# Attention's projection as one direct product by blocks of features, with gating by pairs of heads ahead of it

## Chip, cores and metric

One core of one Trainium2 chip runs the program. The time is device time in microseconds, the median of three runs. The float32 inputs and outputs lie in the chip's memory; every large product is made on TensorE in three parts (high by high, high by low, low by high, "fp32r"), so each operand is split beforehand into a high part (a rounded copy, ScalarE) and a low part (what is left, VectorE or GpSimd).

## Reference

The layer is cut to the part at its end. `y_a` is the MLP branch and `y_b` attention over 8 heads of 128 features:

```python
    y_b = mixture_of_dilations(q, k, v).reshape(B, S, D_B)
    y_b = y_b * jax.nn.silu(z_b)                 # z_b: gating
    m = g_a * (y_a @ w_pa) + g_b * (y_b @ w_pb)  # two projections, [1024 x 2048] and [1024 x 1024]
    return x + rms_norm(m @ w_o, g_post)         # output, [1024 x 1024]
```

Sequence 1024, width 1024. `y_b @ w_pb` is what the change computes in another way.

## The kernel before

The program runs through stages: the norm and V, the other input projections with the MLP's mixing, attention head by head with the MLP's projection interleaved, and a tail. Only the tail is touched.

**Names.** Tiles are 128 partitions by features or tokens. `y` is attention's output times the gate, by features: 8 heads of 128 features (k), two column halves b of 512 tokens. `o_d` holds attention's output and `z_d` the gate in memory, `th_d` the sigmoid gates, `ma_d` the MLP's gated projection, `wo_d` the parts of `w_o` split early. `wh` and `wl` are high and low parts of weights (eight buffers each, `WB`), `wr` raw weights (three buffers). `split` (L158 to L160) makes a high part on ScalarE (ACT) and a low one, on VectorE (DVE) unless told otherwise; `operand` (L103 to L109) does so for weights, low on GpSimd (POOL). `steps` is a generator that issues the rest of the MLP's projection (`pa`, L844 to L846, then `tha` on L850), a quarter of a product at a time.

**The tail before.** Its pool `tail` lies in the memory that attention's pools gave up. `load_y` (L903) loads a quarter of y (four heads, one half, 1 MB) and z in two pieces into `wr` buffers, and multiplies them on POOL (L910). `load_w` loads quarters of `w_pb`. The product is then made from seven smaller ones instead of eight (the Winograd form of Strassen's scheme): sums of quarters of weights and of y (`by_k`, L919, on DVE), seven products of 4 banks x 4 k x 3 matmuls (L1031 to L1033, tiles `pbp`), and corrections between their results (L1041). The operands of product n + 1 are made while product n runs. `gated` (L980 to L988) takes a finished bank: times th on DVE, plus ma on POOL, split into `mh` and `ml`. `load_o` loads the split output weights behind products p5 and p4 and at the end: half of them into y's and the weights' tiles, the others into `wh` and `wl` buffers. The output (L1079 to L1086) runs over pairs of chunks of 128 tokens, with both column halves i of each.

**What sets the order.** Each engine works through its own list in order, and so does SyncE (SP), which issues nearly all transfers: one that waits (for a buffer, or for a store that must land) holds those behind it. The lists come from the order of the code and from a scheduler that may move an instruction past others on its engine; a tile's buffer is given to the next tile once all that read it are done.

Of the kernel before, what the change touches and what calls it, by code (L numbers as in the profile page):

```python
# [36 lines left out]
def tile_hybrid_encoder(  # L37
# [855 lines left out]

    with tc.tile_pool(name="tail", bufs=1) as tp:
        def whole(tag, name, dtype=F32):
            return tp.tile([P, 4, 512], dtype, tag=tag, name=name)


        y, wq, mh, ml = {}, {}, {}, {}

        def load_y(j, b):  # L903
            bs = slice(512 * b, 512 * (b + 1))
            y[j, b] = t = whole(f"y{j}{b}", f"y{j}{b}")
            nc.sync.dma_start(t, o_d[4 * j:4 * j + 4, :, bs].rearrange("k p n -> p k n"))
            for k in range(0, 4, 2):
                z = wpool.tile([P, 2, 512], F32, tag="wr", bufs=3, name=f"zf{j}{b}{k}")
                nc.sync.dma_start(z, z_d[4 * j + k:4 * j + k + 2, :, bs].rearrange("k p n -> p k n"))
                nc.gpsimd.tensor_tensor(t[:, k:k + 2, :], t[:, k:k + 2, :], z, ALU.mult)  # L910

        def load_w(i, j):
            wq[i, j] = whole(f"q{i}{j}", f"pb{i}{j}")
            nc.sync.dma_start(wq[i, j], w_pb[512 * j:512 * (j + 1), 512 * i:512 * (i + 1)].rearrange(
                "(k p) n -> p k n", p=P))

        def by_k(dst, first, second, op, eng=nc.vector):
            for k in range(4):
                eng.tensor_tensor(dst[:, k, :], first[:, k, :], second[:, k, :], op)  # L919
                yield  # L920

        load_y(0, 0)
        load_w(1, 0)
        load_w(1, 1)
        take(steps, 8)
        load_w(0, 0)
        load_y(1, 1)
        s1, s2 = whole("s1", "s1"), whole("s2", "s2")
        for _ in by_k(s1, wq[1, 0], wq[1, 1], ALU.add):
            take(steps, 2)  # L930
        load_y(0, 1)
        load_w(0, 1)
        for _ in by_k(s2, s1, wq[0, 0], ALU.subtract):
            take(steps, 2)
        load_y(1, 0)
        t3 = whole("t3", "t3")
        for _ in by_k(t3, y[1, 1], y[0, 1], ALU.subtract):
            take(steps, 2)
        for _ in by_k(y[0, 1], y[0, 1], y[0, 0], ALU.subtract):
            take(steps, 2)  # L940
        for _ in by_k(wq[1, 0], wq[0, 0], wq[1, 0], ALU.subtract):
            take(steps, 2)
        take(steps)
        u2, u3 = [hpool.tile([P, 4, 512], F32, tag=t, name=f"u{t}") for t in ("r01h", "r10h")]
        for q_, tag in (((0, 0), "r10l"), ((1, 0), "r01l")):
            ml[q_] = hpool.tile([P, 4, 512], F32R, tag=tag, name=f"ml{tag}")
        sso = tp.tile([P, 8, 4], F32, name="sso")


        t2, t1, t4, w_s3, s4 = y[0, 0], y[0, 1], y[1, 0], wq[1, 0], s2  # L950
        TOKENS = {"p1": y[0, 0], "p6": t2, "p2": y[1, 0], "p7": t3, "p5": t1, "p4": t4, "p3": y[1, 1]}
        WEIGHTS = {"p1": wq[0, 0], "p6": s2, "p2": wq[0, 1], "p7": w_s3, "p5": s1, "p4": wq[1, 1], "p3": s4}
        spare = [(0, 0), (1, 1)]

        def tokens_of(n, hl):
            if n == "p6":
                sums = by_k(t2, t3, y[0, 0], ALU.add)
            elif n == "p4":
                sums = by_k(t4, y[1, 0], t2, ALU.subtract)
            else:  # L960
                sums = iter(())
# [54 lines left out]
        for at, (n, _, _) in enumerate(STEPS):  # L1016
# [7 lines left out]
            for u in range(4):  # L1024
                ps = acc.pop((into, u)) if into else next_bank(f"pb{n}{u}")
                if n in ("p1", "p7", "p5"):
                    acc[n, u] = ps
# [108 lines left out]
```

## Time and profile before

| | us |
|---|---|
| median of three runs | 1615.31 |
| the runs | 1612.32, 1615.61, 1615.31 |
| the profiled execution | 1610.12 |
| its span, first to last instruction | 1608.3 |
| mean granted clock of TensorE | 0.976 |

| part of the tail, us from the span's start | from | to |
|---|---|---|
| last of the MLP's projection (TensorE alone on it) | 1358.95 | 1408.78 |
| attention's projection | 1408.78 | 1499.33 |
| output | 1499.33 | 1600.67 |
| last square, scale, sum and store | 1600.67 | 1608.3 |

In rows of a view, an engine stands ahead of its line of the code, the operation and what it writes and reads; "[... <-X]" is the time that the engine sat idle before, and what ended it. PE is TensorE, SPq the time in which SP held a transfer's instruction.

### The profile page before, as it was taken

The page shows a single profiled execution, that of the slowest core. Times are in us where ns is not written, and L with a number is a line of the kernel's source. Part 1 is how long each engine was busy: PE and PEld are TensorE (multiplying, and loading weights), DVE is VectorE, ACT ScalarE, POOL GpSimd, SP SyncE. Part 2 cuts the span into 40 slices and gives each one's busy share as a digit, 9 for nine tenths or more (in the row PEclk, how much of TensorE's full clock was granted, in tenths as well). Part 3 has the DMA queues.
Part 4 walks back from the last instruction along what each step waited for, and adds up shares of the span by engine and source line. Part 5 has one row for each costly group of instructions (what it writes and reads, how often), then busy time and mean ns, then how long its engine had stood idle before and what let it go on. Part 6 is the DMA issues. An engine that isn't in the chain of part 4 may idle for free.

```text
span 1608.3 us, 22594 instructions
## 1 busy us (share of the span) xinstructions
PE 1508.8 (94%) x7751; PEld 1264.2 (79%) x7751; DVE 934.6 (58%) x1698; ACT 716.0 (45%) x1391; POOL 818.5 (51%) x723
## 2 busy tenths in 40 slices
PE   8959999999999999999999999989998899789798
PEld 4747999988888888788788888767877777677586
DVE  5852544476675765757565655566666554596412
ACT  5422533343433434443354544677776665144111
POOL 3542644465555555565555555364344433687432
PEclk8979999999999999999999999999999999999899
DMA  8335433334534443536243343676666665924631
GB/s 263 136 125 191 150 106 105 111 125 133 162 125 144 135 147 116 180 102 193 99 159 130 121 148 110 217 227 196 194 198 179 207 188 168 334 97 144 235 105 66
DMA packets 238467, 252.14 MB, mean 157 GB/s; under 512 B 14056, under 2 KB 174856, under 8 KB 238096
## 3 DMA queue, kind: packets, MB, share of 16 engines
q1 hardware_dynamic: 238128, 250.14, 48.8%
q8 instruction: 61, 1.00, 0.3%
q10 hardware_dynamic: 224, 0.56, 0.1%
q14 instruction: 54, 0.44, 0.1%
HBM read 174.10 MB, written 76.55 MB: 156 GB/s over the span
## 4 chain that ended last, share of the span: by engine, by line
PE 63%; DVE 13%; DMA 6%; ACT 6%; issue 6%; POOL 5%; SPq 1%; DVEq 0%; POOLq 0%; ACTq 0%
PE sg L515 2%; PE pa L845 1%; PE pa L844 1%; PE pa L846 1%; DMA wr_pa<-in_w_proj_a_dram 1%; DMA vn<-v_d 1%; DVE vn L504 1%; PE vb L154 1%; PE vb L156 1%; PE vb L155 1%; PE sc L650 1%; ACT st L657 1%; DVE y L919 1%; ACT qrh L159 1%; PE pr L731 1%
## 5 line engine op out<-in xcount | busy, mean ns | idle before, releaser
L108 POOL TENSOR_TENSOR wl_pa<-wr_pa,wh_pa 128x512 fp32r<-128x512 f32 x56 | 73.4, 1318 | 86.7 <-ACT wh_pa L106 69.4
L504 DVE TENSOR_SCALAR vn<-vn,mean,rstd 128x128 f32<-128x128 f32 x128 | 55.3, 486 | 34.9 <-DMA vn<-v_d 34.5
L657 ACT ACTIVATE st<-st,own 128x256 f32<-128x256 f32 (+1 forms) x128 | 63.0, 493 | 24.0 <-DVE own L653 23.4
L106 ACT ACTIVATE wh_pa<-wr_pa 128x512 fp32r<-128x512 f32 x64 | 38.7, 624 | 46.1 <-DMA wr_pa<-in_w_proj_a_dram 37.2
L671 POOL COPY oth<-own 32x4 f32<-32x4 f32 x128 | 25.1, 196 | 54.1 <-ACT st L657 49.8
L653 DVE CUSTOM_DVE_ANT_0 st<-sc,tb 128x256 f32<-128x256 f32 x64 | 25.6, 422 | 37.8 <-PE sc L652 27.4
L160 POOL TENSOR_TENSOR vl<-vn,vh 128x512 fp32r<-128x512 f32 x32 | 41.3, 1292 | 0.8 <-ACT vh L159 0.8
L1085 ACT ACTIVATE sq<-o 128x512 f32<-128x512 f32 x16 | 9.6, 599 | 70.5 <-PE o L1083 70.5
L160 POOL TENSOR_TENSOR qcl<-q,qch 128x512 fp32r<-128x512 f32 x16 | 24.8, 1552 | 29.7 <-ACT qch L159 29.6
L1061 DVE TENSOR_TENSOR sso<-sso 128x1 f32<-128x1 f32 x8 | 1.3, 159 | 63.5 <-ACT sq L1085 63.5
L159 ACT ACTIVATE mhp<-mb 128x512 fp32r<-128x512 f32 x16 | 10.1, 632 | 54.9 <-POOL mb L987 54.9
L160 DVE TENSOR_TENSOR vl<-vb,vh 128x512 fp32r<-128x512 f32 x16 | 10.8, 688 | 38.2 <-ACT vh L159 33.9
L165 POOL TENSOR_TENSOR sso<-sso,mhalf 128x1 f32<-128x1 f32 x8 | 4.4, 552 | 54.9 <-DVE sso L164 54.9
L108 POOL TENSOR_TENSOR wl_wos<-wr_wos,wh_wos 128x512 fp32r<-128x512 f32 x16 | 20.7, 1293 | 22.8 <-ACT wh_wos L106 22.8
L154 PE MATMUL vb<-wh_vb,hT00h 128*128 128x512 f32 x32 | 14.2, 445 | 18.7 <-DVE vl L160 18.7
L1081 PE MATMUL o<-woh,mhp 128*128 128x512 f32 x64 | 26.3, 414 | 5.8 <-DMA woh<-wo_h 5.8
L987 POOL TENSOR_TENSOR mb<-thb,mb 128x512 f32<-128x512 f32 x16 | 21.4, 1337 | 19.8 <-DVE thb L986 15.5
L160 DVE TENSOR_TENSOR ptla<-pa,ptha 128x512 fp32r<-128x512 f32 (+1 forms) x32 | 19.8, 618 | 17.7 <-ACT ptha L159 17.6
L910 POOL TENSOR_TENSOR y<-y,zf 128x1024 f32<-128x1024 f32 x8 | 24.0, 3006 | 11.5 <-DMA zf<-z_d 8.7
L1082 PE MATMUL o<-wol,mhp 128*128 128x512 f32 x64 | 26.8, 422 | 3.1 <-DMA wol<-wo_l 3.1
L650 PE MATMUL sc<-krh,qch 128*128 128x256 f32 (+2 forms) x80 | 24.3, 306 | 5.7 <-DVE own L653 5.2
L653 DVE CUSTOM_DVE_ANT_0 st<-sc,ta 128x256 f32<-128x256 f32 x48 | 20.0, 420 | 15.2 <-PE sc L652 7.3
(2695 smaller groups left out, 6073.0 us busy)
## 6 DMA issues: line engine op xcount, KB each, us to landing
wr_pa<-in_w_proj_a_dram SPq DMA_DIRECT2D x32, 512.0 KB, 5.4
wr_g<-in_w_in_dram SPq DMA_DIRECT2D x16, 512.0 KB, 3.8
wr_va<-in_w_in_dram SPq DMA_DIRECT2D x16, 512.0 KB, 3.8
wr_u<-in_w_in_dram SPq DMA_DIRECT2D x16, 512.0 KB, 3.7
wr_z<-in_w_in_dram SPq DMA_DIRECT2D x16, 512.0 KB, 4.2
vn<-v_d SPq DMA_DIRECT2D x32, 256.0 KB, 3.1
y_d<-s SPq DMA_DIRECT2D x32, 256.0 KB, 2.5
wr_yf<-y_d SPq DMA_DIRECT2D x16, 512.0 KB, 5.1
```

What stands on the lines that cost most here:

```text
L106: nc.scalar.activation(hi, src, AF.Copy)
L108: low.tensor_tensor(lo, src, f32(hi), ALU.subtract)
L154: nc.tensor.matmul(ps, lhs[k][0], rh, start=(k == 0), stop=False)
L159: nc.scalar.activation(hi, src, AF.Copy)
L160: low.tensor_tensor(lo, src, f32(hi), ALU.subtract)
L504: nc.vector.tensor_scalar(vn[:, c, :], vn[:, c, :], mean[:, 4 * b + c, 0:1], rstd[:, 4 * b + c:4 * b + c + 1], op0=ALU.subtract, op1=ALU.mult)
L515: nc.tensor.matmul(pg[:, 256 * c:256 * (c + 1)], w[:, 2 * cp + c, :], wst, start=(w is vh and c == 0), stop=(w is vl and c == 1), skip_gro ...
L650: nc.tensor.matmul(dst, lhs[0], rhs[0], start=True, stop=False)
L653: nc.vector.tensor_tensor_reduce(st[:, t, :n], ps[:, t, :n], bias, -1.0, -NEG, ALU.add, ALU.min, own[:, half, idx, 0:1])
L657: nc.scalar.activation(st[:, t, :n], st[:, t, :n], AF.Exp, bias=own[:, half, idx, 0:1], scale=-1.0, accum_out=own[:, half, idx, 1:2])
L1081: nc.tensor.matmul(ps, mhi, wh, start=(k == 0), stop=False)
L1082: nc.tensor.matmul(ps, mhi, wl, start=False, stop=False)
```

## The change

The seven products become one direct product, by blocks of 128 output features (m = 0 to 7) and two column halves: 16 banks of 8 k x 3 matmuls. The weights of a block are loaded whole (8 x 128 x 128, rows of 128 columns) by `cols_block`, one block ahead in the code. Ahead of it, `gated_heads` loads o and z for two heads and one half, multiplies on POOL head by head, and splits into tiles of one head each; 16 such steps alternate with four steps of the MLP each. The tiles of o have two buffers, that of z one. The output's first three chunks of weights for column half 0 have tiles of their own; the other five take `wh` and `wl` buffers, and those of half 1 the y tiles of b = 0. The output's loop goes by token half b, then i, then four chunks. The low part of `m` is made on DVE throughout, and the very last store is issued from ACT's queue.

```diff
-        def load_y(j, b):
...
-            y[j, b] = t = whole(f"y{j}{b}", f"y{j}{b}")
-            nc.sync.dma_start(t, o_d[4 * j:4 * j + 4, :, bs].rearrange("k p n -> p k n"))
-            for k in range(0, 4, 2):
-                z = wpool.tile([P, 2, 512], F32, tag="wr", bufs=3, name=f"zf{j}{b}{k}")
...
-                nc.gpsimd.tensor_tensor(t[:, k:k + 2, :], t[:, k:k + 2, :], z, ALU.mult)
...
+        def gated_heads(h, b):
+            bs = slice(512 * b, 512 * (b + 1))
+            o, z = [tp.tile([P, 2, 512], F32, tag=t, bufs=n, name=f"{t}{h}{b}") for t, n in (("o", 2), ("z", 1))]
+            for t, src in ((o, o_d), (z, z_d)):
+                nc.sync.dma_start(t, src[h:h + 2, :, bs].rearrange("k p n -> p k n"))
+            for i in range(2):
+                y[h + i, b] = [tp.tile([P, 512], F32R, name=f"y{s}{h + i}{b}") for s in "hl"]
+                nc.gpsimd.tensor_tensor(o[:, i, :], o[:, i, :], z[:, i, :], ALU.mult)
+                split(*y[h + i, b], o[:, i, :])
                 yield
...
+        ready = (_ for h in range(0, H, 2) for b in range(2) for _ in gated_heads(h, b))
+        for i in range(16):
+            take(ready, 1)
+            take(steps, 4)
+            if i == 8:
+                take(steps, 8)
         take(steps)
...
+                if i == 0 and k > 2:
+                    wo[i, k] = [wpool.tile([P, 512], F32R, tag=f"w{s}", bufs=WB, name=f"wo{s}{k}") for s in "hl"]
                 else:
+                    wo[i, k] = [tp.tile([P, 512], F32R, tag=f"y{s}{k}0" if i else f"wo{s}{k}", name=f"wo{s}{i}{k}")
+                                for s in "hl"]
...
+        wb[0] = cols_block(w_pb, 0, 0, "pb0")
+        for m in range(KT):
+            if m + 1 < KT:
+                wb[m + 1] = cols_block(w_pb, (m + 1) * P, 0, f"pb{m + 1}")
+            if m == 4:
+                load_o(0, range(3))
+            elif m == 7:
+                load_o(0, range(3, KT))
+            for b in range(2):
...
+                ps = next_bank(f"pb{b}{m}")
+                for k, (lh, ll) in enumerate(wb[m]):
+                    rh, rl = y[k, b]
+                    nc.tensor.matmul(ps, lh, rh, start=(k == 0), stop=False)
+                    nc.tensor.matmul(ps, lh, rl, start=False, stop=False)
+                    nc.tensor.matmul(ps, ll, rh, start=False, stop=(k == KT - 1))
+                nc.vector.tensor_tensor(th, th, ps, ALU.mult)
+                nc.gpsimd.tensor_tensor(ma, th, ma, ALU.add)
+                split(*[t[:, m % 4, :] for t in m_[m // 4][b]], ma)
+        load_o(1, range(KT))
...
-        for cc in range(4):
...
+        for b in range(2):
             for i in range(2):
-                for c in (2 * cc, 2 * cc + 1):
...
+                for c in range(4 * b, 4 * b + 4):
```

Left out of it are the removed loads of quarters, sums, products and corrections (`load_w`, `by_k`, `tokens_of`, `weights_of`, `begin`, `gated`) and lines that differ only in names.

How the instructions stand on SP where the tail's loads begin, behind the last stores of attention. Before (names: `y` and `zf` are quarters of o and their gates, `pb` quarters of `w_pb`, `pa161` the MLP's weights; DMAHW is a transfer that must have landed):

```order
L906 DMA y00_13530<-o_d_86 128x4x512 [waits DMAHW6_49,DMAHW0_49,PE_49]
L914 DMA pb10_13538<-in_w_proj_b_dram 128x4x512 [waits DMAHW2_49]
L914 DMA pb11_13540<-in_w_proj_b_dram 128x4x512 [waits DMAHW3_49]
L914 DMA pb00_13578<-in_w_proj_b_dram 128x4x512 [waits DMAHW4_49]
L906 DMA y11_13580<-o_d_86 128x4x512 [waits DMAHW5_49]
L909 DMA zf110_13582<-z_d_91 128x2x512 [waits DMAHW7_49,Pool_49]
L909 DMA zf112_13585<-z_d_91 128x2x512 [waits Pool_49]
L113 DMA wr_pa161_13604<-in_w_proj_a_dram 128x8x128 [waits Pool_49]
```

And of the change, from the same place:

```order
L903 DMA o00_13530<-o_d_86 128x2x512 [waits DMAHW6_49,DMAHW0_49,PE_49]
L903 DMA z00_13531<-z_d_91 128x2x512 [waits DMAHW2_49]
L903 DMA o01_13580<-o_d_86 128x2x512 [waits DMAHW3_49]
L113 DMA wr_pb0_13855<-in_w_proj_b_dram 128x8x128 [waits DMAHW4_49,Pool_49]
L903 DMA z01_13581<-z_d_91 128x2x512 [waits DMAHW5_49,DMAHW2_49,Pool_49]
L903 DMA o20_13632<-o_d_86 128x2x512 [waits DMAHW1_49,DVE_49]
L851 DMA ma_d_95<-tha14_13562 128x512 [waits DMAHW7_49,DVE_49]
L113 DMA wr_pb1_13865<-in_w_proj_b_dram 128x8x128 [waits Pool_49]
L903 DMA z20_13633<-z_d_91 128x2x512 [waits DMAHW5_49,Pool_49]
```

The loads of pa161 and pa171 now stand ahead of the first o; every z from the second on waits for POOL.

On POOL, in the change, around the last pair of heads (`o60` and `o61` are the products for heads 6 and 7, halves 0 and 1; `mb00` adds the MLP's part to the first bank):

```order
L906 TENSOR_TENSOR o41_13790<-o41_13790,z41_13791 128x512
L108 TENSOR_TENSOR wl_pb3_0_14021<-wr_pb3_14017,wh_pb3_0_14019 128x512 [waits DMAHW3_49,PE_49,Activation_49]
L108 TENSOR_TENSOR wl_pb3_1_14025<-wr_pb3_14017,wh_pb3_1_14023 128x512 [waits PE_49,Activation_49]
L906 TENSOR_TENSOR o60_13818<-o60_13818,z60_13819 128x512 [waits DMAHW5_49,DMAHW0_49,DVE_49]
L906 TENSOR_TENSOR o60_13818<-o60_13818,z60_13819 128x512
L962 TENSOR_TENSOR mb00_13877<-thb00_13875,mb00_13877 128x512 [waits DVE_49]
L906 TENSOR_TENSOR o61_13832<-o61_13832,z61_13833 128x512 [waits DMAHW4_49,DMAHW1_49,Pool_49]
```

`mb00`, which needs the whole first bank, stands ahead of the products for heads 6 and 7 of the second half; two low parts of weights stand between pairs. Before, POOL's products y (L910) stood among the low parts of `pa` and `pbp`.

On SP, the output's weights. Before (`woh` and `wol` are high and low parts; `thb` and `mb` belong to the last banks):

```order
L1003 DMA woh3_14452<-wo_h_97 128x512 [waits DMAHW6_49,PE_49]
L1003 DMA wol3_14453<-wo_l_98 128x512 [waits DMAHW7_49,PE_49]
L983 DMA thb010_14471<-th_d_92 128x512 [waits DMAHW0_49,Pool_49]
L985 DMA mb010_14473<-ma_d_95 128x512 [waits DMAHW1_49,Pool_49]
L983 DMA thb011_14492<-th_d_92 128x512 [waits DMAHW2_49,Pool_49]
L985 DMA mb011_14494<-ma_d_95 128x512 [waits DMAHW3_49,DVE_49]
L1003 DMA woh4_14542<-wo_h_97 128x512 [waits DMAHW4_49,PE_49]
```

And of the change, at its last two banks (`woh10` is half 1, chunk 0; `woh00`, the first of half 0, stands 43 rows further up, behind the first th of the second block):

```order
L952 DMA thb07_14429<-th_d_92 128x512 [waits DMAHW3_49,Pool_49]
L938 DMA woh7_14425<-wo_h_97 128x512 [waits DMAHW4_49,PE_49]
L938 DMA wol7_14426<-wo_l_98 128x512 [waits DMAHW5_49,PE_49]
L954 DMA mb07_14431<-ma_d_95 128x512 [waits DMAHW6_49,DVE_49]
L938 DMA wol10_14496<-wo_l_98 128x512 [waits DMAHW7_49,PE_49]
L938 DMA woh10_14495<-wo_h_97 128x512 [waits DMAHW0_49,PE_49]
L952 DMA thb17_14462<-th_d_92 128x512 [waits DMAHW1_49,Pool_49]
L954 DMA mb17_14464<-ma_d_95 128x512 [waits DMAHW2_49,DVE_49]
```

The weights of half 0 have moved from behind the last product to between the banks of the blocks.

More of the change, by code (lines that the diff above doesn't have):

```diff
@@ L912, in load_w @@
[L912 to L919, printed above, removed]
-                yield
[L922 to L940, printed above, removed]
@@ L947, in tile_hybrid_encoder @@
         sso = tp.tile([P, 8, 4], F32, name="sso")
[L950 to L961, printed above, removed]
-            for k in range(4):
-                take(sums, 1)
-                split(hl[0][:, k, :], hl[1][:, k, :], TOKENS[n][:, k, :])
-                yield
@@ L967, in weights_of @@
-        def weights_of(n, res):
-            if n == "p3":
-                take(by_k(s4, wq[0, 1], s2, ALU.subtract))
-            for u in range(4):
-                res.append(operand(WEIGHTS[n][:, :, u * P:(u + 1) * P], f"pb{n}{u}"))
-                yield
-        def begin(n):
-            hl, res = quarter(*spare[0], f"pb{n}"), []
-            spare.reverse()
-            return hl, res, tokens_of(n, hl), weights_of(n, res)
-        def gated(i, b, u, c):
-            bs = slice(512 * b, 512 * (b + 1))
-            th = wpool.tile([P, 512], F32, tag="th", bufs=2, name=f"thb{i}{b}{u}")
-            nc.sync.dma_start(th, th_d[8 + 4 * i + u][:, bs])
-            ma = wpool.tile([P, 512], F32, tag="ws", bufs=2, name=f"mb{i}{b}{u}")
-            nc.sync.dma_start(ma, ma_d[4 * i + u][:, bs])
-            nc.vector.tensor_tensor(th, th, c, ALU.mult)
-            nc.gpsimd.tensor_tensor(ma, th, ma, ALU.add)
-            split(mh[i, b][:, u, :], ml[i, b][:, u, :], ma, nc.vector if u % 2 else nc.gpsimd)
@@ L1054, in tile_hybrid_encoder, with load_o @@
-        load_o(0, range(4, 8))
-        gp = whole("y11", "gp")[:, 0:2, :].rearrange("p k n -> p (k n)")
+        wo = {}
+        def load_o(i, ks):
+            for k in ks:
+                if i == 0 and k > 2:
+                    wo[i, k] = [wpool.tile([P, 512], F32R, tag=f"w{s}", bufs=WB, name=f"wo{s}{k}") for s in "hl"]
+                else:
+                    wo[i, k] = [tp.tile([P, 512], F32R, tag=f"y{s}{k}0" if i else f"wo{s}{k}", name=f"wo{s}{i}{k}")
+                                for s in "hl"]
+                for s in range(2):
+                    nc.sync.dma_start(f32(wo[i, k][s]), wo_d[s][i, k])
@@ L1060, in out_last @@
             nc.sync.dma_start(x_, x_t[c])
+            out_ = tp.tile([P, D], F32, tag="o", bufs=2, name=f"out{c}")
             nc.vector.tensor_tensor(sso[:, c, 2:3], sso[:, c, 0:1], sso[:, c, 1:2], ALU.add)
```

90 lines of the change are left out of this document (16 added, 74 removed).

## The prediction

> **What bounds the kernel now.** I read the page first, then the tail of the program stage by stage, the waits of TensorE (PE) there, and the timeline around the longest of them.
>
> ```profile
> span 1608.3 us, 22594 instructions
> PE 1508.8 (94%) x7751; PEld 1264.2 (79%) x7751; DVE 934.6 (58%) x1698; ACT 716.0 (45%) x1391; POOL 818.5 (51%) x723
> ```
>
> PE bounds the whole, so the tail is counted in matmuls and in the time that PE loses. Nothing before the tail is changed. The stages, on PE: the end of the MLP projection (the first two rows, split where its waits begin), attention's projection, and the output (the last two).
>
> ```profile
> core 0: us, PE busy (x), PEclk, DMA share, GB/s
> 1358.95:1380.73 21.78, 21.78 (x98) 1.00 0.79 281
> 1380.73:1408.78 28.05, 19.66 (x73) 0.88 0.92 313
> 1408.78:1499.33 90.55, 81.65 (x337) 0.96 0.40 131
> 1499.33:1525.00 25.67, 16.85 (x52) 0.80 0.74 259
> 1525.00:1600.67 75.67, 75.66 (x334) 1.00 0.24 80
> ```
>
> ```profile
> 1358.96 0.39 PE L844 MATMUL pa<-ya1000h,wh_pa 128*128 128x512 f32 x1
> 1380.51 0.39 PE L846 MATMUL pa<-ya1111h,wl_pa 128*128 128x512 f32 x1
> ...
> 1393.63 0.79 PE L846 MATMUL pa<-ya1201h,wl_pa 128*128 128x512 f32 x1 [5.13 <-POOL wl_pa L108]
> 1394.22 0.63 PE L844 MATMUL pa<-ya1201h,wh_pa 128*128 128x512 f32 x1
> 1397.64 0.57 PE L846 MATMUL pa<-ya1201h,wl_pa 128*128 128x512 f32 x1
> ...
> 1600.28 0.39 PE L1083 MATMUL o<-woy,mlp 128*128 128x512 f32 x1
> ```
>
> The first two rows are the first and last of 96 matmuls in a row (8 groups of 12): 21.55 us over 95 steps, 0.2268 us each. From 1394.22 to 1397.64, behind the wait of 5.13 us, eight steps take 3.42 us, 0.43 each: after a long wait PE runs at half speed for some 4 us, so it costs about 2 us more than its length.
>
> By the code 168 matmuls of the MLP are left at 1358.95, then come 336 (7 products x 4 x 4 x 3) and 384 (16 banks x 8 x 3). At 0.2268 these need 38.1, 76.2 and 87.1 us and take 49.8, 90.6 and 101.3, so the stages lose 11.7, 14.4 and 14.2: **40.3 us**. Who causes it:
>
> ```profile
> engine line waited for: us in total, times, longest us
> PE pa L846 <- POOL wl_pa L108: 5.8, 2, 5.1
> PE o L1081 <- DMA woh<-wo_h: 5.8, 4, 2.8
> PE pbp L1032 <- DVE pbp500l L160: 3.2, 3, 1.8
> PE o L1082 <- DMA wol<-wo_l: 3.1, 2, 2.7
> PE pbp L1032 <- DVE pbp200l L160: 2.8, 4, 0.7
> PE pa L844 <- ACT wh_pa L106: 2.6, 2, 1.3
> ```
>
> MLP: a late weight operand. Projection: low parts that VectorE (DVE) makes between its sums. Output: late weights. The rest of each loss is half speed behind these waits.
>
> **The change, part by part.** It adds 384 - 336 = 48 matmuls: +10.9 us. It can take away at most the 40.3. What it puts in their place is decided in the gating stage.
>
> *MLP end.* What PE waited for was a load stuck behind others:
>
> ```profile
> 1359.94 0.38 SPq L113 DMA_DIRECT2D wr_pa<-in_w_proj_a_dram  x1
> 1360.38 0.57 SPq L791 DMA_DIRECT2D o_d<-o  x1
> 1365.31 0.37 SPq L906 DMA_DIRECT2D y<-o_d  x1
> 1375.46 0.92 SPq L113 DMA_DIRECT2D wr_pa<-in_w_proj_a_dram  x1
> ```
>
> The zf loads took `wr` buffers, so SyncE's queue (SP) held the weights of pa161 until 1375.46 and of pa171 longer. Now z has its own buffer; both loads are issued ahead of the first heads, pa171 where the first row stands (its buffer comes free when POOL ends pa160's low part). All 168 matmuls then run on to about 1397, 1398 with the two banks that wait for DVE's th products queued behind low parts of y (up to 1 us).
>
> *Gating.* 8 pairs of heads and column half, each a load of o and of z (512 KB each), two POOL products, two ScalarE (ACT) high parts, two DVE low parts. o has two buffers, **z has one**: each z load waits on SP until both POOL products of the pair before are done, so pairs cannot overlap. The prices:
>
> ```profile
> xr<-in_x_dram SPq DMA_DIRECT2D x8, 512.0 KB, 3.6
> wr_pa<-in_w_proj_a_dram SPq DMA_DIRECT2D x32, 512.0 KB, 5.4
> wr_yf<-y_d SPq DMA_DIRECT2D x16, 512.0 KB, 5.1
> zf<-z_d SPq DMA_DIRECT2D x8, 512.0 KB, 12.3
> ...
> DMA packets 3190, 4.88 MB, mean 376 GB/s; under 512 B 102, under 2 KB 1049, under 8 KB 3189
> ```
>
> ```profile
> L987 POOL TENSOR_TENSOR mb<-thb,mb x16: 1259/1287/1739, 1446.3 to 1518.0; 128x512 f32<-128x512 f32 x16
> L986 DVE TENSOR_TENSOR thb<-thb,pbp x4: 672/676/689, 1445.6 to 1454.9; 128x512 f32<-128x512 f32 x4
> L159 ACT ACTIVATE ya1310h<-wr_yf x4: 613/614/615, 1276.3 to 1284.1; 128x512 fp32r<-128x512 f32 x4
> L160 POOL TENSOR_TENSOR ya0310l<-wr_yf,ya0310h x2: 1346/1547/1748, 1067.9 to 1069.2; 128x512 fp32r<-128x512 f32 x2
> L160 DVE TENSOR_TENSOR ya0310l<-wr_yf,ya0310h x2: 681/1050/1419, 1067.4 to 1068.4; 128x512 fp32r<-128x512 f32 x2
> ```
>
> (Columns of the first fence: KB each, median us to landing; its last row is the traffic from 1372 to 1385. Of the second: min/median/max ns.) xr is a load of this size on a quiet queue, 3.6. zf's 12.3 came behind 5 MB of y and pb; now o, a block of w_pb and one store or two, some 1.3 MB, go out just behind each z, 3.5 us at 376 GB/s, and are through before the next z. A product is 1.29, up to 1.75 beside DVE. So a cycle is 3.6 + 0.15 for two hand-overs + two products of 1.29 to 1.75: 6.3 to 7.2; I take 6.5, near the undisturbed row, since o's low part can touch only the second product.
>
> The first o goes out at 1365.31, as y does now (it waits for the same store of head 7); z right behind lands at 1365.31 + 3.6 + 0.52 MB at 376 GB/s (1.4) = 1370.3; products end at 1372.9. Pair 7 of 8 (heads 6, 7, first half) ends 6 cycles later, **1411.9**. PE, having eaten six heads by 1402, stands still about 9 us. ACT 0.7, DVE 0.7 to 1.4 and the last matmuls at half speed end bank 1 at 1414.6. On POOL the product mb of that bank stands ahead of the last pair: DVE 0.8, POOL 1.4, two products 2.6, ACT and DVE 1.8, matmuls 0.7: bank 2 ends at 1421.9. (The 18 matmuls of bank 2 that need no late head take 4.1 us, at half speed at most 7.7, and lie inside these 7.3 within half a microsecond: at most +0.5, taken at nothing.) z's last load, 1411.9 + 3.6 = 1415.5, is under that cover; without it, it would be the wait.
>
> Behind a waiting z on SP stand the next o, two ma_d stores, two th loads and blocks of w_pb; PE wants these not before 1397, and o's wait is shorter than z's. POOL makes two low parts of weights between pairs, 2.6 inside the 3.6 of a load: hidden; at 1.75 each POOL would need 4 x 1.75 = 7.0 per cycle and set it.
>
> On a product beside DVE: the Trainium skill, SBUF — State Buffer, "SBUF: two separate sides", calls the pair of ports that DVE and GpSimd share an exclusive lock, which the instruction that starts first holds to its end. By it the second product, starting right behind the first, is not lengthened: cycle 6.35, the sum below 0.9 us better; by the 1748 ns row in every pair it is 6.8, and 1.8 worse.
>
> *Rest of the projection.* 336 matmuls. Per bank (24 matmuls, 5.4 us) DVE does 0.7 + 0.7, POOL 1.3 (+ 1.3 of weights), ACT 0.6 (+ 0.6): all beside PE, with 8 banks in turn. The 32 sums and 20 corrections on DVE, and 12 token and 12 weight splits, go: no wait of PE's hangs on them any more. 76.2 us, to 1498.1.
>
> *Output.* The first three chunks of weights have own buffers and five take weight buffers that PE frees from chunk 4 on, 10 us or more ahead; the second half's go into y's tiles, wanted 4 x 5.4 us after the start. I cost its waits at nothing (now 14.2); 384 matmuls, 87.1, end at 1585.2. Today they end at 1600.28 + 0.23 = 1600.5. The closing (last square, scale, add, store: 7.8 us to 1608.3) keeps its steps; its last store moves to ACT's queue, plus or minus 0.3.
>
> **Sum**: -11.7 + 1 (MLP), +10.9 matmuls, projection's loss 14.4 replaced by 1421.9 - 1398 - 48 x 0.2268 = 13.0, output -14.2: -15.4; the dates say 1585.2 - 1600.5 = -15.3. The profiled execution took 1610.1 (span 1608.3), so it becomes 1594.8. It lies 5.2 under the median of the three runs, 1615.3 (1612.3 to 1615.6); from the median: **1600.0**.
>
> **Rivals.**
>
> *Slower: z's buffer paces everything at over 9 us.* Mechanism: z loads land late, queued behind o and the 512-byte rows of w_pb. Break-even is 15.3 / 6 = 2.55 us more per cycle: 9.05, a landing of 6.1. For: wr_pa lands in 5.4, zf in 12.3. Against: in the order of SP each z stands ahead of the next traffic. At a landing of 7 and 1.5 a product, 10.2: +6.9, 1622.
>
> *In between, the same.* Landing 5.1, products 1.75: 8.75, 13.5 back: 1613.5.
>
> *The output's waits stay* (the weights are not there earlier): 14 of the 15 go: 1614. For: SP holds them between th and mb loads that wait on POOL. Against: the buffers are free a chunk and more ahead.
>
> *The chain is hidden better*: no wait at all would give 10.9 - 40.3 = -29, 1586; POOL alone (5.2 a cycle) would allow 1592; but the load stands in the chain, and no row above has one under 3.6.
>
> **How the numbers follow.** Forecast (cycle 6.2 to 7.2, other waits up to 5 us): 0.64, own range 1594 to 1606. Better than that 0.10; a slower chain, but under 1612, 0.12; the same, by either rival, 0.07; slower 0.07. About 0.2%, 3 us, is what a measurement of this kernel can tell from no change. Faster: 0.64 + 0.10 + 0.12 = 0.86; same 0.07; slower 0.07. Range 1590 to 1611.
>
> **What would show it.** Right: z loads about 6.5 us apart from 1365 to 1412; no wait of the MLP's matmuls on wl_pa; one PE wait of about 9 us on ACT or DVE for heads 6, 7, then about 1 to 2 on the last pair; no wait from there to the end; output's first matmul near 1498. Wrong: z landings over 5, POOL products at 1.7 throughout, any wait of o on woh or wol, waits on wl_pb, or a clock below 0.95 after 1425.

## The result and the profile after

| | before | after |
|---|---|---|
| median of five runs, us | 1613.26 | 1598.73 |
| the runs | 1612.32 to 1615.61 | 1597.55 to 1606.56 |
| profiled execution, span | 1610.12, 1608.3 | 1604.17, 1602.4 |
| ratio | | 0.9921, 95% interval 0.9893 to 0.9948 |

Faster by 0.8%. The profiled execution of after is one of its slower ones, so the two traces can't be laid over each other by date. Where the MLP's last groups begin and no instruction has changed yet, after already lies 5.0 us later: the first load of o goes out at 1370.33, that of y at 1365.31 before. From that load on I count, in all that follows: **from it to the end the kernel before takes 243.0 us, the changed one 232.1**, 10.9 less.

The page of after, its first lines:

```profile
span 1602.4 us, 22610 instructions
...
PE 1512.4 (94%) x7799; PEld 1273.2 (79%) x7799; DVE 872.7 (54%) x1642; ACT 702.2 (44%) x1363; POOL 783.7 (49%) x711
```

PE has 48 matmuls more (7799 for 7751); DVE, which loses the sums, is busy 62 us less (934.6 before). The stages of after on PE, as they were shown of before (the middle two rows are the projection, split behind its second bank):

```profile
core 0: us, PE busy (x), PEclk, DMA share, GB/s
1363.90:1405.73 41.83, 38.68 (x170) 1.00 0.74 223
1405.73:1431.15 25.42, 14.79 (x51) 0.80 0.83 252
1431.15:1506.86 75.71, 75.71 (x335) 1.00 0.65 209
1506.86:1594.50 87.64, 87.64 (x385) 1.00 0.26 92
1594.50:1602.40 7.90, 0.21 (x1) 0.81 0.31 116
```

The first row, the MLP's 168 matmuls, took 49.8 before: 8.0 less. The projection is 101.1 (90.6 before, with 48 matmuls fewer): 10.6 more. The output, 87.6, had 101.3: 13.7 less. In the last two full stages PE is busy in every microsecond at a granted clock of 1.00; all idle time stands in the first two rows. The waits of PE from 1355 on name it:

```profile
PE pb L958 <- ACT yh L159: 9.8, 1, 9.8
PE pa L844 <- DVE tha L850: 3.1, 2, 1.7
PE pb L959 <- DVE yl L160: 0.8, 2, 0.5
```

No wait on wl_pa or wh_pa, none on the output's weights. Two are new: 3.1 us for the gates of the MLP's last banks, and one of 9.8 us for the high part of a late pair of heads. On PE's timeline that wait is followed by matmuls at half pace (nine steps from 1421.15 to 1425.16 take 4.01 us, 0.45 each, where 0.227 is the full pace):

```profile
1420.04 0.79 PE L958 MATMUL pb<-yh,wh_pb 128*128 128x512 f32 x1 [9.84 <-ACT yh L159]
1421.15 0.79 PE L959 MATMUL pb<-yl,wh_pb 128*128 128x512 f32 x1 [0.32 <-DVE yl L160]
...
1425.16 0.47 PE L959 MATMUL pb<-yl,wh_pb 128*128 128x512 f32 x1
```

What that pair waited for is read from SP's timeline; the issues of z:

```profile
1370.33 0.37 SPq L903 DMA_DIRECT2D o<-o_d  x1
1370.75 0.46 SPq L903 DMA_DIRECT2D z<-z_d  x1
...
1379.88 0.36 SPq L903 DMA_DIRECT2D z<-z_d  x1
...
1393.56 0.36 SPq L903 DMA_DIRECT2D z<-z_d  x1
...
1413.57 0.36 SPq L903 DMA_DIRECT2D z<-z_d  x1
...
1420.58 0.37 SPq L903 DMA_DIRECT2D z<-z_d  x1
```

and from POOL's, which shows what releases each of them:

```profile
1377.32 2.53 POOL L906 TENSOR_TENSOR o<-o,z 128x512 f32<-128x512 f32 x2 [3.20 <-issue]
...
1390.99 2.54 POOL L906 TENSOR_TENSOR o<-o,z 128x512 f32<-128x512 f32 x2 [1.30 <-issue]
1393.48 3.45 POOL L108 TENSOR_TENSOR wl_pb<-wr_pb,wh_pb 128x512 fp32r<-128x512 f32 x2
1397.47 2.54 POOL L906 TENSOR_TENSOR o<-o,z 128x512 f32<-128x512 f32 x2 [0.54 <-DMA z<-z_d]
...
1418.06 2.49 POOL L906 TENSOR_TENSOR o<-o,z 128x512 f32<-128x512 f32 x2 [0.77 <-issue]
```

Products from 1390.99 to 1393.53, the next z out at 1393.56, its products at 1397.47: each load goes out 0.03 us behind the products of the pair before. Between 1379.88 and 1420.58 lie six issues, 6.78 us apiece. POOL's low parts of weights, 3.45 for two, lie inside the load. That reads like the chain that the prediction described, but a row of POOL that is nearly full (2.54 + 3.45 = 6.0 of 6.78) reads like a bound of POOL too, and the traces alone do not decide between them. Nor do they say which part of the change took the output's waits away.

### The profile page after: what moved, and what is told of

Same layout as the page of the kernel before. It is cut to its first block, busy times and chain, and to the rows that moved or that the text cites. A ratio compares the mean times of both kernels' runs of the same rounds, so it can differ in the third digit from the quotient of the medians.

```text
span 1602.4 us, 22610 instructions
## 1 busy us (share of the span) xinstructions
PE 1512.4 (94%) x7799; PEld 1273.2 (79%) x7799; DVE 872.7 (54%) x1642; ACT 702.2 (44%) x1363; POOL 783.7 (49%) x711
## 5 line engine op out<-in xcount | busy, mean ns | idle before, releaser
L958 PE MATMUL pb<-yh,wh_pb 128*128 128x512 f32 x128 | 50.9, 398 | 9.8 <-ACT yh L159 9.8
L959 PE MATMUL pb<-yl,wh_pb 128*128 128x512 f32 x128 | 51.1, 399 | 0.8 <-DVE yl L160 0.8
L960 PE MATMUL pb<-yh,wl_pb 128*128 128x512 f32 x128 | 50.5, 395 | 0.0
L160 DVE TENSOR_TENSOR yl<-o,yh 128x512 fp32r<-128x512 f32 x16 | 18.2, 1137 | 39.1 <-ACT yh L159 38.4
L958 PEld LDWEIGHTS pb<-yh,wh_pb 128*128 128x128 f32 x128 | 24.6, 192 | 15.4 <-ACT yh L159 10.3
L160 DVE TENSOR_TENSOR vl<-vb,vh 128x512 fp32r<-128x512 f32 x16 | 10.8, 688 | 39.3 <-ACT vh L159 35.4
L959 PEld LDWEIGHTS pb<-yl,wh_pb 128*128 128x128 f32 x128 | 24.5, 192 | 7.5 <-DVE yl L160 2.4
```

The costliest lines, as they stand in the source:

```text
L160: low.tensor_tensor(lo, src, f32(hi), ALU.subtract)
L958: nc.tensor.matmul(ps, lh, rh, start=(k == 0), stop=False)
L959: nc.tensor.matmul(ps, lh, rl, start=False, stop=False)
L960: nc.tensor.matmul(ps, ll, rh, start=False, stop=(k == KT - 1))
```

## The experiments

**Theory A**: the one buffer of z paces the gating; TensorE stands still for the pair that its next bank needs last; the MLP's end and the output gain what was forecast, each by its own cause. Against it: B, POOL's own work paces; C, the transfers do; G, the output is quicker by its new buffers beside y. Twelve kernels ran, in three sets, each set on a chip of its own and with the kernel before in it. Times are medians; "tail" is from the first load of o (or y) to the end, in the kernel's trace; MLP, projection and output are its parts (to the first matmul of the next stage; the closing is counted with the output).

| kernel | time, us | ratio to before, interval | MLP | projection | output | tail |
|---|---|---|---|---|---|---|
| before | 1613.26 | 1 | 43.5 | 90.6 | 109.0 | 243.0 |
| after | 1598.73 | 0.9921, 0.9893 to 0.9948 | 35.4 | 101.1 | 95.5 | 232.1 |
| after_again | 1603.57 | 0.9945, 0.9926 to 0.9965 | 35.2 | 101.3 | 95.5 | 232.0 |
| low_dve | 1600.83 | 0.9924, 0.9907 to 0.9941 | 35.2 | 101.0 | 95.8 | 232.0 |
| z2 | 1601.09 | 0.9930, 0.9914 to 0.9946 | 46.0 | 90.1 | 95.2 | 231.4 |
| z2_low_dve | 1601.97 | 0.9931, 0.9915 to 0.9947 | 46.8 | 89.3 | 95.6 | 231.7 |
| z2_early | 1592.16 | 0.9890, 0.9873 to 0.9908 | 33.0 | 95.7 | 95.2 | 223.9 |
| b_first | 1588.15 | 0.9854, 0.9834 to 0.9873 | 35.0 | 87.0 | 95.5 | 217.6 |
| wo_ring | 1599.16 | 0.9926, 0.9913 to 0.9940 | 35.0 | 101.0 | 94.9 | 230.8 |
| before_zown | 1609.91 | 0.9991, 0.9979 to 1.0004 | 31.7 | 100.5 | 109.5 | 241.7 |
| pairs_b | 1604.55 | 0.9941, 0.9924 to 0.9958 | 35.1 | 104.7 | 95.5 | 235.2 |
| wo_behind | 1603.36 | 0.9937, 0.9918 to 0.9957 | 35.0 | 102.4 | 97.1 | 234.5 |
| b_first_z2e | 1586.53 | 0.9831, 0.9815 to 0.9848 | 32.8 | 89.0 | 95.2 | 217.0 |
| b_first2 | 1587.07 | 0.9830, 0.9811 to 0.9850 | 34.9 | 87.0 | 95.5 | 217.4 |

### after_again: how large is the change itself?

No edit.

> The changed kernel once more, unaltered, as the ruler for the three that run beside it, and as a second trace of the tail. Theory A (the one z buffer paces the gating: each pair's z is issued when the products of the pair before are done) expects the spacing of the z issues again near 6.8 us (6.5 behind pairs without a w_pb block ahead, 7.1 to 7.2 behind those with one), one wait of about 10 us on TensorE for the high part of pair 6, no wait in the output, and 238.5 us from the point of the MLP at which the two kernels part to the end, within 1 us. The 5.0 us by which the first trace lay later than that of before when the tail began should not be a property of the kernel: the first part, which is the same program, should come out anywhere within 5 us of it. If it were a property (rival: other addresses in memory), the tail would begin again near 1370 us.

Tail 232.0, as in the first trace (232.1), one wait of 10.1 on yh, 3.0 for the MLP's gates, none in the output; its z issues are 6.8 us apart on average again. The tail begins at 1367.25 instead of 1370.33, and that of b_first at 1366.21 in one trace and 1372.27 in the other. So where the tail begins differs by up to 6 us between executions of one program, and how long it lasts by 0.1 or 0.2. (The two traces of b_first are from two chips; but the five executions of after in one set already spread over 9.0 us.) For this kernel the tail is the better ruler: the change is worth 11 us there. The two medians of after are 14.5 and 9.2 below those of before in their sets, and lie on both sides of it.

### low_dve: does POOL pace the pairs?

```
-        wb[0] = cols_block(w_pb, 0, 0, "pb0")
+        wb[0] = cols_block(w_pb, 0, 0, "pb0", nc.vector)
...
-                wb[m + 1] = cols_block(w_pb, (m + 1) * P, 0, f"pb{m + 1}")
+                wb[m + 1] = cols_block(w_pb, (m + 1) * P, 0, f"pb{m + 1}", nc.vector if m < 4 else nc.gpsimd)
```

(The last argument is the engine that makes the low parts.)

> The low parts of w_pb's first five blocks on VectorE in place of GpSimd; z keeps its one buffer. Theory A: GpSimd's low parts (3.45 us a cycle) lie beside the load of the next z (3.7 to 4.4 us), so taking them away frees nothing: cycle 6.4 to 6.8 as before, at most 0.3 us less in each of six, and a time between the changed kernel's and 2 us below. Rival B (GpSimd's own work paces): the cycle falls toward 2.5 us and whatever the load needs beside it, 4 us or more less in all six cycles together for each 0.7 us that a cycle loses. Rival D (VectorE becomes late: ten more low parts of 0.7 to 1.6 us, ahead of the low parts of y and of the MLP's gates): up to 5 us slower, and the wait on TensorE is then for yl or the gates of the MLP.

POOL's timeline, with the low parts of w_pb gone from it:

```profile
1388.74 2.54 POOL L906 TENSOR_TENSOR o<-o,z 128x512 f32<-128x512 f32 x2 [0.96 <-DVE wl_pb L108]
1395.19 2.54 POOL L906 TENSOR_TENSOR o<-o,z 128x512 f32<-128x512 f32 x2 [3.92 <-DMA z<-z_d]
1402.68 2.53 POOL L906 TENSOR_TENSOR o<-o,z 128x512 f32<-128x512 f32 x2 [4.95 <-DMA z<-z_d]
...
1416.03 2.49 POOL L906 TENSOR_TENSOR o<-o,z 128x512 f32<-128x512 f32 x2 [4.31 <-DMA z<-z_d]
```

From the second row on POOL stands idle 4 to 5 us before each pair, until z lands, and the pairs come no faster: (1416.03 - 1388.74) / 4 = 6.8. Tail 232.0. B falls, and so does D: VectorE's ten low parts cost nothing. An engine that is busy 6.0 of 6.8 us was not the bound; what was ends the idle time that appears once the work is taken away, here "DMA z".

### z2 and z2_low_dve: a second buffer for z, and a lesson on order

```
-            o, z = [tp.tile([P, 2, 512], F32, tag=t, bufs=n, name=f"{t}{h}{b}") for t, n in (("o", 2), ("z", 1))]
+            o, z = [tp.tile([P, 2, 512], F32, tag=t, bufs=n, name=f"{t}{h}{b}") for t, n in (("o", 2), ("z", 2))]
...
-                if i == 0 and k > 2:
+                if i == 0 and k > 1:
```

(An output chunk's own buffers pay for it, and the loads of the output's chunks are split accordingly; z2_low_dve adds the edit of low_dve.)

> Two buffers for z in place of one, and two output chunks beside y in place of three, which pays for it. Theory A (the z load stands in the chain: 3.7 to 4.4 us landing, 0.15, then two products of 2.5 us = 6.8 us a pair): the load of the next pair now runs beside the products, and the cycle falls to what GpSimd has to do in it, two products of 2.5 and two low parts of 3.45 = 6.0 us. Six cycles, 0.8 us each: pair 6 ends 4.7 us earlier, TensorE's wait of 9.8 falls to about 5, and the time falls by 4 to 5 us. Rival B (GpSimd's order paces the pairs, since its low parts of the weights stand between the products and take 3.45 us for certain): the cycle stays at 6.5 or more, within 1.5 us of the time of the changed kernel. Rival C (the transfers pace: o, z and w_pb share the engines, and two z at once land later): spacing of the products unchanged, time the same or up to 2 us slower.

> Both edits together. Theory A: with the load beside the products and the low parts off GpSimd, a cycle is bound by transfers alone: 1 MB of o and z and half a MB of w_pb, 1.5 MB at the 285 to 376 GB/s that the first loads showed = 4.2 to 5.5 us instead of 6.8. Pair 6 ends 8 to 15 us earlier, TensorE's 9.8 us for it shrink to between 0 and 2, the half speed behind it goes too (some 2 us), and the time is 7 to 11 us below the changed kernel's; what then ends TensorE's waits is the MLP's gates (3.1 us). Rival B (GpSimd paces by its low parts only): as low_dve. Rival D (VectorE late): the gain of z2 alone, 4 to 5 us, or less.

In neither does the time move: tail 231.4 and 231.7. Taken alone that would speak for C. The waits of PE in z2 say otherwise:

```profile
PE pb L958 <- ACT wh_pb L106: 12.8, 1, 12.8
...
```

The wait on heads is gone; there is a longer one on the first block of w_pb. SP's timeline of z2 shows why:

```profile
1401.92 3.20 SPq L903 DMA_DIRECT2D z<-z_d  x2
...
1406.57 0.46 SPq L113 DMA_DIRECT2D wr_pb<-in_w_proj_b_dram  x1
```

The first load of w_pb goes out behind the last z, at 1406.57, 37 us behind the first load of o; in after it was 1.5 us behind. With one buffer, z's waits had left room on SP for w_pb's blocks, and the scheduler had put them there; with two it put all of z first. The pairs themselves did get faster (POOL's timeline of z2, first and seventh pair):

```profile
1375.87 2.54 POOL L906 TENSOR_TENSOR o<-o,z 128x512 f32<-128x512 f32 x2 [2.53 <-issue]
...
1406.96 2.48 POOL L906 TENSOR_TENSOR o<-o,z 128x512 f32<-128x512 f32 x2 [2.22 <-DMA z<-z_d]
```

The seventh starts 31.1 us behind the first, 40.7 in after (1377.32 and 1418.06 above). So the failure was in my expectation, which left out that the freed chain takes the place of the weights.

### z2_early: the same with the weights put back between the pairs

```
         for i in range(16):
             take(ready, 1)
             take(steps, 4)
...
+            if i in AT:
+                wb[AT.index(i)] = cols_block(w_pb, AT.index(i) * P, 0, f"pb{AT.index(i)}")
```

AT is (9, 11, 13); the same three blocks are left out of the later loop.

> Two buffers for z again, but with the first three blocks of w_pb placed between the gating pairs in the program, since in the run with two buffers they all went out behind the last z (the first at 1406.6 instead of 1368.7) and TensorE waited 12.8 us for the first block's high part in place of 9.8 for the heads. Theory A (z's load stood in the chain; the gain was eaten by the weights, which the z loads had let past before): the wait on wh_pb goes, TensorE waits for pair 7 of 8 only, which ended at 1409.5 with two buffers and would now end some 1.5 us later (half a MB more ahead of it): a wait of 4 to 6 us. The time falls by 4 to 7 us below the changed kernel's. Rival B (the weights' transfers cost the chain what the second buffer brings, since o, z and w_pb share the engines): the wait is 8 us or more, the time within 2 us of the changed kernel's.

Tail 223.9, 8.1 below after, and the waits of PE:

```profile
PE pb L959 <- ACT yh L159: 5.0, 1, 5.0
PE pa L844 <- DVE tha L850: 0.6, 1, 0.6
...
```

The wait on heads fell from 9.8 to 5.0, as A had it; the rest is the MLP's gates, which are no longer late (33.0 for the MLP in place of 35.4), and less half speed. B and C would have given nothing. **The single buffer of z does set the pace.** What the other 5 us hang on no run tried, but POOL's timeline of z2_early points to POOL itself (sixth and seventh pair):

```profile
1399.42 2.54 POOL L906 TENSOR_TENSOR o<-o,z 128x512 f32<-128x512 f32 x2
1403.22 2.49 POOL L108 TENSOR_TENSOR wl_pb<-wr_pb,wh_pb 128x512 fp32r<-128x512 f32 x2 [1.26 <-ACT wh_pb L106]
1405.66 2.49 POOL L906 TENSOR_TENSOR o<-o,z 128x512 f32<-128x512 f32 x2
```

The pairs are 6.2 us apart, and in these rows POOL does not wait for z: it waits 1.26 us for ACT's high part, makes two low parts of w_pb, and goes straight on to the next products. So rival B, wrong for the changed kernel, may be the next bound once z has two buffers; that is a reading of the trace, not a test.

### b_first and pairs_b: which pair does TensorE want?

b_first leaves z alone and turns the order round, of the pairs and of the banks:

```
-        ready = (_ for h in range(0, H, 2) for b in range(2) for _ in gated_heads(h, b))
+        ready = (_ for b in range(2) for h in range(0, H, 2) for _ in gated_heads(h, b))
...
-        for m in range(KT):
+        for m, b in [(m, b) for g in (0, 4) for b in range(2) for m in range(g, g + 4)]:
```

(b, which was the inner loop, goes; the loads of later blocks stand behind the banks whose buffers they take.)

> The changed kernel with its order by column halves: first the four pairs of the first half are gated, then the four of the second; and of the projection's blocks of features 0 to 3 the first half's banks come first, then the second half's, then the same for blocks 4 to 7. No instruction is added or left out, z keeps its one buffer. Theory A (TensorE waits because every bank needs the last pair of heads of its half, and the chain of z reaches pair 7 of 8 only some 50 us after the first load): the first half is through after four pairs, 1374 + 3 x 6.8 + 2.5 = 1397 in the last trace, before the MLP ends at 1402; the four banks of the first half give TensorE 21.8 us more, to 1424, and the chain ends at about that time. The wait of 10 us and the half speed behind it go, the MLP's waits of 3 us stay and are no longer hidden behind the 10: the time falls by 8 to 12 us below the changed kernel's. Rival E (TensorE's idle time there is wanted by something else too, w_pb's operands above all, of which four blocks are needed in the first 22 us in place of two): a new wait on wh_pb or wl_pb of 5 us or more, and a gain under 5. Rival F (the single z was never the cause, the transfers were): the chain takes as long, pair 8 later than 1430, and the gain is again under 5.

The stages of b_first on PE, from the first load of o: MLP, projection, output, closing.

```profile
1366.21:1401.25 35.04, 32.26 (x141) 1.00 0.79 241
1401.25:1488.29 87.04, 87.04 (x385) 1.00 0.82 266
1488.29:1575.97 87.68, 87.68 (x385) 1.00 0.24 80
1575.97:1583.80 7.83, 0.16 (x1) 0.74 0.31 115
```

The projection takes 87.04 us for 384 matmuls, 0.2267 each, without a gap and at full clock; it was 101.1. The only wait of PE that is left in the tail is one on tha, 2.8 us in two pieces. Tail 217.6, 14.5 below after, 2.5 more than the most expected. Of it the projection has 14.1: the 9.8 and 0.8 of waits, and a remainder of 3.5 in place of the 2 that I had put down for half speed; 2.6 of it stand in the eleven steps behind the long wait in after (1420.04 to 1425.46, less 0.3 of wait). (The median, 1588.15, is over four executions, one of which took 7282 us, of which more below; the three others took 1585.6 to 1589.8.) The chain of z is as slow as ever (its issues are 6.9 us apart); it is no longer looked for so soon. So rival E falls, and F with it.

pairs_b takes the first of the two lines alone.

> Only one of the two halves of the kernel b_first (1588.2 us, no wait left on the heads): the pairs are gated first half first, but the banks of the projection alternate between the halves as in the changed kernel. Theory A (what TensorE waits for is the pair that its next bank needs last): the first bank finds its four pairs ready and has no wait, the second needs the last pair of all, which ends 3 or 4 us after the first half's last one in the changed kernel, so the wait moves from the first bank to the second, in three or four pieces of 2 to 4 us, 10 to 13 in all, and the time stays within 3 us of the changed kernel's (from the first load of o to the end 229 to 234 us, where the changed kernel has 232.0 and b_first 217.6). Rival I (the gain of b_first came from the order of the gating or its loads, not from the banks): 8 us or more below the changed kernel, and no wait over 4.

Waits of PE in pairs_b:

```profile
PE pb L958 <- ACT yh L159: 9.9, 3, 5.1
PE pa L844 <- DVE tha L850: 2.5, 2, 1.8
PE pb L959 <- DVE yl L160: 1.3, 3, 0.6
```

As A had it, the 10 us are there again, in three pieces ahead of pairs 6 to 8, on the second bank. Rival I falls: the order of the gating alone gains nothing. The tail is even 3.2 us above after's, a little outside the range that I gave, though the waits on yh sum to the same. The stage shows what the pieces cost (the first 32.6 us of the projection; the first fence is pairs_b, the second after_again):

```profile
1402.42:1435.00 32.58, 21.40 (x67) 0.69 0.70 224
```

```profile
1402.44:1435.00 32.56, 22.10 (x82) 0.79 0.78 243
```

15 matmuls fewer in the same time, 3.4 us. Of these 0.7 are more idle time (32.58 - 21.40 against 32.56 - 22.10), the rest is pace, at a granted clock of 0.69 in place of 0.79: on PE's timeline the matmuls behind each of the three waits start 0.43 us apart, and 10 us in three pieces cost more than in one.

### before_zown: what is the MLP's end worth by itself?

The kernel before, with z in the buffer of t3, which is not in use yet:

```
+            zt = whole("t3", f"zf{j}{b}")
             for k in range(0, 4, 2):
-                z = wpool.tile([P, 2, 512], F32, tag="wr", bufs=3, name=f"zf{j}{b}{k}")
+                z = zt[:, k:k + 2, :]
```

> The kernel before, with its z loads in a buffer of their own (the one of t3, which is not yet in use) in place of the ring of raw weights; its products, sums and orders stay. Theory A (at the MLP's end TensorE waited for w_pa blocks whose buffers z had taken): the waits on wl_pa and wh_pa (8.4 us, 11.7 with half speed) fall to under 2. What is gained there is kept only as far as the projection's first tokens are ready earlier too: with one buffer for a block of four heads its cycle is two products of 2.6 and a load of 4 to 5 us = 10 us, so block 4 of 4 is done 40 us after the first load, at 1410, and the first bank (block 1 only) is not held. By A the time is 6 to 11 us below the kernel before. Rival H (the projection's order of sums and splits is late all the same): the MLP ends earlier and TensorE waits as much more on yl, pb or the sums: within 3 us of the kernel before.

Its stages on PE, in the same order:

```profile
1366.84:1398.52 31.68, 31.68 (x141) 1.00 0.75 274
1398.52:1499.01 100.49, 82.18 (x337) 0.93 0.51 171
1499.01:1600.67 101.66, 92.25 (x385) 0.95 0.36 125
```

The MLP ends without a gap, 11.8 us sooner than before, counted from the first load: the cause and the size that the prediction gave (11.7) are shown. But the projection takes 9.9 us more, and the tail falls by 1.3 only; the ratio's interval holds 1. The waits moved:

```profile
PE pbp L1032 <- ACT pbp611h L159: 7.0, 1, 7.0
...
PE pbp L1033 <- DVE pbp100l L160: 6.0, 3, 2.4
```

A's 6 to 11 us fall, and the time is where rival H put it: time won at the MLP's end is lost to the next thing that is late, in this kernel as in after. That this is H's cause alone is not shown, for the edit delays something itself: z has one tile for four heads where the ring had three for two heads each, and POOL ends the products of the third block of y 40.1 us behind the first load (1406.89), 34.8 before (1400.12). Product p6 (`pbp6`), where the 7.0 stand, needs that block; product p1 (`pbp1`), where 6.0 are lost, does not.

### wo_ring and wo_behind: what took the output's waits away?

wo_ring sends all eight chunks of the output's first half through the ring of weight buffers; wo_behind keeps the own buffers of three and sends chunks 3 to 7 behind the second half's eight.

```
-                if i == 0 and k > 2:
+                if i == 0:
```

```
-            elif m == 7:
-                load_o(0, range(3, KT))
...
-        load_o(1, range(KT))
+        with tc.issue_after(load_o(1, range(KT))):
+            load_o(0, range(3, KT))
```

(`load_o` now returns its last transfer, and `issue_after` holds what follows behind it.)

> The changed kernel without own buffers for the output's first three chunks: all eight of the first half go through the ring of weight buffers, where they wait for w_pb's blocks, and the second half's stay beside y. Asks which part of the change took the output's waits away. Theory A (the own buffers matter little: what helps is that the ring comes free bank by bank, over 20 us before the output, and that the second half's chunks have y's buffers): at most the last chunk is late, and seven chunks of products, 4.8 us, stand ahead of it: 0 to 2 us slower than the changed kernel. Rival G (the buffers beside y are what removed the waits): TensorE waits on woh or wol again, as before by 9 us and 14 with half speed, and the kernel loses 5 to 14 us.

> The changed kernel with the order of the output's weights turned round: chunks 3 to 7 of the first half go out behind all eight of the second half, as most of the second half's stood ahead of the first's in the kernel before. Own buffers, sizes and everything else stay. Theory J (what took the output's waits away is the order and date of the issues on SyncE: the first half's ring chunks go out from 25 us before the output on, where before the last twelve issues came after 1498 us, one us before it): now 16 issues of 0.47 us and 4 MB at 376 GB/s, 11 us, stand ahead of them, chunk 7 lands some 10 us after the projection's end in place of being there, its products end 5 to 6 us later than without a wait, and with half speed the kernel loses 5 to 9 us, as waits of the first output bank on woh or wol. Rival G (own buffers for the first three chunks and y's for the second half do it, whatever the order): no wait over 1 us in the output and at most 1 us lost.

wo_ring loses nothing: 94.9 for output and closing (95.5), and no wait of the output. So the buffers beside y were not needed for it, and G as I put it falls. wo_behind loses 1.6 in the output and 2.4 in the tail, below the 5 to 9 that J gave and above the 1 that G allowed, with one wait on PE:

```profile
PE o L989 <- DMA woh<-wo_h: 1.4, 1, 1.4
```

though chunk 3 goes out 1.9 us after the output's first matmul (1506.92), and chunk 7 9.0 after it (SP's timeline, the first and last of the ten issues):

```profile
1508.79 0.32 SPq L938 DMA_DIRECT2D woh<-wo_h  x1
...
1515.88 0.32 SPq L938 DMA_DIRECT2D wol<-wo_l  x1
```

That the loss is so small lies in the order on PE: 29 matmuls stand there now ahead of the wait, 9 each of three banks, which need chunks 0 to 2 only, and two more, where after has 24 of one bank. Three chunks in own buffers and several open banks cover some 6.6 us (29 x 0.2268). So in the new loop either cover goes most of the way by itself: early issues without own buffers (wo_ring, nothing lost), or own buffers with issues up to 9.0 us late (wo_behind, 1.6 lost). The kernel before had neither. Its last woh on SP's timeline,

```profile
1516.31 0.38 SPq L1003 DMA_DIRECT2D woh<-wo_h  x1
```

went out 17.0 us into the output (from 1499.33), but which of its waits on SP held that load I did not try to undo. Nor did any run put back the old loop, which turned to the second half's weights after two chunks of tokens (48 matmuls, 10.9 us) and not after four. By the dates it would hardly have mattered in after, which is an estimate: the last load of that half goes out 1.5 us into the output (1508.40), and no transfer of woh or wol took over 6.5 in that stretch.

### b_first_z2e and b_first2: the best version

The first joins b_first and z2_early, the second is b_first again.

> The two edits that helped, together: order by column halves, and two buffers for z with w_pb's first blocks placed between the pairs. Theory A: in b_first the chain of z was off TensorE's path already, so a faster chain has only the MLP's two waits (2.8 us, VectorE's products behind the low parts of y) to act on; those fell to 0.6 where z had two buffers. The time is 0 to 4 us below b_first's (from the first load of o to the end 214 to 217.6). Rival F (the load chain still costs TensorE something that its waits do not name): 5 us or more below.

> The kernel b_first once more, unaltered, beside the three others, since one of its executions took 7282 us, over four times as long as all others, and left it three that can be compared. Expected: 1585 to 1591 us in every execution and 217.6 us from the first load of o to the end, within 1 us. If the long one belongs to the kernel (rival: an order in which a queue can block for milliseconds), it shows again in one of some five.

Tails of 217.0 and 217.4, ratios of 0.9831 and 0.9830: the second buffer of z brings nothing once the order hides the chain. It takes the MLP's gates from 2.5 to 0.9 and puts 1.2 us of waits on wl_pb in their place. The b_first kernel is the better of the two, being the smaller edit: 1587.07 against 1612.79 for the kernel before in its set, 1.7% faster, about twice the gain of the change studied. The five executions of b_first2 took 1583.7 to 1591.5, a little wider than the 1585 to 1591 that I expected. The one of 7282 us did not come back among them; its cause is not known, and nothing in the traces bears on it.

## Why the prediction came out as it did

The forecast was 1600.0, the median is 1598.7, and the mechanism is the one described: one wait on the heads of pair 7 of 8, then half speed, then no wait to the end. But in the tail the kernel gained 10.9 us, not 15.3; that the median came out so close is luck, because the part ahead of the tail, in which nothing is changed, varies by more than the 4.4 us between them. By its steps, from the first load of o:

- **48 matmuls more, +10.9**: right. b_first shows the price bare: 87.04 for 384.
- **MLP's end**: the cause was right (before_zown: 11.8 without z in the ring of weights, 11.7 forecast). The price of what comes after it, "up to 1 us" for two banks behind VectorE's low parts, was too small: 3.1 us of waits, the MLP ending 35.4 us behind the first load of o instead of 32.7. It costs after nothing, since PE then waits 9.8 us for the heads all the same; in b_first it is the last wait left.
- **First pair**: products due 5.0 us behind the first load started 7.0 behind it: mis-sized by 2.0. I let one o go ahead of z00, but o01 and a block of w_pb went out right behind, and all four were under way together; that this is what made it late no run tested.
- **Cycle 6.5**: 6.78, six times 0.28 = 1.7 us. The products were not the reason: two took 2.49 to 2.54 in each of the first seven pairs, though VectorE's low parts fell beside them. The landing was: 3.7 or 4.4 us where I took 3.6. (A cycle of 6.8 stands in the prediction too, for products of 1748 ns; that it is close to what was measured is a coincidence.) With the first pair this puts pair 7's end 50.2 us behind the first load where 46.6 was forecast.
- **Product beside DVE**: of the two readings weighed there, the one by which the second product is not lengthened is borne out. The Trainium skill, SBUF — State Buffer, "SBUF: two separate sides", has DVE and GpSimd take their shared ports by a lock that the holder keeps to its end; 2.54 us for two products agrees, and so do the low parts of y beside them, which took VectorE 691 ns at the quickest and 1556 at the slowest:

```profile
L160 DVE TENSOR_TENSOR yl<-o,yh x16: 691/1099/1556, 1379.3 to 1429.4; 128x512 fp32r<-128x512 f32 x16
```

- **Second bank** 10.0 behind pair 7: 10.6 (1420.55 to 1431.15). **Rest of the projection** 76.2: 75.7. **Output** 87.1 without waits: 87.6, right, though the reason given was half right: the early issues carry it alone, the own buffers were not needed (wo_ring). **Closing**: 7.9 for 7.8.

So the sum missed by 2.0 + 1.7 + 0.6 on the chain; the others, -0.5, +0.5 and +0.1, cancel: 4.4. The rival "the chain is better hidden", 1586 to 1592, was priced about right and judged by the wrong question: I asked whether the chain could be faster, and it was the order of its use that hid it (b_first, 1587 to 1588). And before_zown, as far as it can be read, points to an error of the method: I listed the MLP's end as a gain of its own, yet a term ahead of a chain whose date is set elsewhere is no gain. That the sum came out right all the same is because the projection was then dated by the chain, not by adding.

## What to carry to other kernels

Where a chain of loads feeds a stage, ask first what the consumer wants earliest, and order the chain and the consumer's loop by that; here this was worth 14 us, a second buffer 8, and both together no more than the first. When an edit lets one queue's waits go, look at what the scheduler had put into them: in z2 the freed loads passed the weights, and a gain of 10 us on the chain became a wait of 12.8 for something else. And measure a local change from a point in the program that it can't move, since the part ahead of it may vary by more than half of what it is worth, as here by 6 us of 11.

## What the runs showed of the hardware that was not expected

- Two traces of the same program (b_first and b_first2, on two chips) begin their tail 6.1 us apart (1366.21 and 1372.27), and the tails agree within 0.2 us of 217.5.
- Three waits of 1.1, 5.1 and 3.8 us, 9.9 in all, let 15 matmuls (3.4 us) fewer through than one of 10.1, by 0.7 us of other idle time and by the clock granted behind them: 0.69 against 0.79 over 32.6 us.
- A z load of 512 KB lands in 3.7 us or in 4.4, in two rows of after's issues, taken around the sixth and the seventh z. The second had a load of w_pb, whose rows are 512 bytes, going out 3.2 us ahead of it (1410.42 and 1413.57); no run took that load away, so that it is the cause is only argued. The eighth z (1420.58) landed in 4.4 as well, and no block of w_pb had gone out ahead of it since 1410.42, though one followed 0.9 us behind it.

```profile
z<-z_d SPq DMA_DIRECT2D x1, 512.0 KB, 3.7
z<-z_d SPq DMA_DIRECT2D x1, 512.0 KB, 4.4
```
